# One layer of a hybrid RWKV-7 and S5 network: GELUs ordered behind placed copies, and four smaller reorderings

## The chip, the core and the metric

The kernel runs on one core of a Trainium2 chip. The core has five engines, each with its own queue of instructions that it works off in order: TensorE (PE; its weight loads, PEld, overlap its matmuls), VectorE (DVE), ScalarE (ACT), GpSimd (POOL) and SyncE (SP). Here POOL and SP mostly issue DMAs. The metric is the device time of one execution in microseconds. Lines such as L752 are lines of the kernel before.

## The reference, cut to what matters

One layer for 1024 tokens of width 1024, in float32:

```python
h = rms_norm(x, g_mix_pre)
p = h @ w_in                      # RWKV r, k, v and low ranks | S5 input u | two gates
A = rwkv7_branch(p[rwkv])         # state S per head of 64, one step per token:
#   S = S*w + (S a) b^T + v k^T ;  y = S r ;  then head norm, the bonus (r.k.r_k) v, gate
B = s5_branch(p[u])               # 32 groups of 16 channels, 64 complex states, scan over time
#   y = gelu(Re(C s) + D u) ;  y * sigmoid(y @ w_glu + b_glu)
m = sigmoid(gA) * (A @ w_br0) + sigmoid(gB) * (B @ w_br1)
x = x + rms_norm(m @ w_out, g_mix_post)
z = rms_norm(x, g_ffn_pre) @ w_up           # then a causal convolution of width 3
out = x + rms_norm((gelu(gate) * val) @ w_down, g_ffn_post)
```

## The kernel before

All matrices are multiplied in three matmuls per product: the float32 operands are split into a high part (a cast to fp32r, on ACT) and the rest (a subtraction, on DVE), and PE adds high x high, low x high and high x low (L180 to L182). One such group of three, of 128x128 weights on 512 columns, is called a step here. Weights come by DMA into `wf`, and `wh` (L160, ACT) and `wl` (L161, DVE) are their two parts; activations are split in the same way into `hh` and `hl` (L245, L246).

The stages follow one another: the opening (two halves of 512 tokens are loaded, normalised and multiplied for the S5 input, to about 60 us), the S5 scans in four batches beside the rest of the input projection (to 270), the RWKV recurrence in four groups beside gates, the merge and the GLU (to 740), the rest of the mixing and its norms (to 900), the up-projection (to 1290) and the down-projection.

The order on PE is written out. `drive()` runs several generators ("lanes") against a clock of stated times, `self.now`: each `yield` states what the piece just emitted costs and after how long its next piece is ready. When no lane is ready, the next step of the background work (`fill`: gate tiles, merge, GLU, output projection) is emitted. A stated time that is larger puts more fill ahead of the next piece; it does not itself make the chip wait. On the other engines a scheduler decides by priorities, and `add_manual_dep(..., ORDER)` forces one instruction to stand behind another on the same engine.

The places that the change touches:

- The S5 batch (`s5_batch`, L643 to L655): DVE scans the states, which it holds as `z` and `rot`, and PE then sums three matmuls for each of eight groups (L651 the inputs, L652 and L653 the states). The stated time ahead of them is 17.0 for the first batch and 13.0 for the others (L648).
- The Gram products of a group (`rwkv_front`, L745 to L755; two lanes, u = 0 and 1): 32 small matmuls each into two PSUM banks (L752), masked by DVE into `gr` (L754). `self.masked` is a stated time that keeps the lanes from emitting them too close together. At the end of a front one matmul sums for the bonus (L763), DVE multiplies it (L764), and it uses the same rotating banks.
- The inverse of the chunks' triangular matrices (`rwkv_inv`, L810 to L822): DVE eliminates row by row, the result goes to DRAM (`xd`, L815) and back into `gr` (L822) by DMAs that POOL issues.
- The level (`rwkv_level`, L824 to L851), which puts together blocks of 32 into blocks of 64: DVE transposes `gr` (L835), PE multiplies for u = 0 and 1 (L838), ACT copies the results (L839), PE multiplies again (L840), and ACT copies into `gr` (L841). The chain over the tokens' chunks (L870 to L913) begins behind it.
- The merge's GELUs (`s5_y`, L1250 to L1257): POOL issues the load of an S5 result (L1253), ACT applies GELU (L1254) and casts the high part (L1261), DVE subtracts (L1262). They are forced to stand behind `self.squared`, which is the last square that a front emitted (L700). A load of ACT's function table stands ahead of the first of them.
- The opening (`start`): ACT and DVE split the eight tiles of half 0 as they are normalised (L1046, L245, L246), PE multiplies them (L1158), and the weights of the next S5 columns are split meanwhile.
- The end (`down`, L1895 to L1906): of the last eight output tiles, four are summed with the residual on PE: `resid_sum` multiplies the residual by the identity into a bank (L1898), `outputs` adds the scaled tile (L1829, L1831), and ACT copies it out (L1832). The other four are added by DVE (L1729).

Of the kernel before, what the change touches and what calls it, by code (L numbers as in the profile page):

```python
# [73 lines left out]
class Kern:  # L74
# [546 lines left out]
    def s5_batch(self, b, d, ys):  # L621

        nc, V, G, A = self.nc, self.nc.vector, self.nc.gpsimd, self.nc.scalar
        s = self.s5
        mm = nc.tensor.matmul
        ca, cb, cs, sn, toep, wT = (d[n] for n in ("ca", "cb", "cs", "sn", "toep", "wT"))

        u8 = self.u8[b]
        z = self.t4(shape=(128, 8, 128))
        G.memset(z[:, :, 0:1], 0.0)  # L630
        rot = self.t4(shape=(128, 8, 128))
        yield 0, T_US
        p1, p2 = (self.chk().rearrange("p (g n) -> p g n", n=128) for _ in range(2))
        for p, o in ((p1, 0), (p2, 1)):
            for g in range(8):
                mm(p[:, g], wT[:, g, o:o + 2, :], u8[:, g, :], start=g % 4 == 0, stop=True, skip_group_check=True)
        r2 = self.t4(shape=(128, 8, 128))
        V.tensor_tensor(rot, p1, cs, ALU.mult)
        V.tensor_tensor(r2, p2, sn, ALU.mult)
        V.tensor_tensor(rot, rot, r2, ALU.add)  # L640
        for g in range(8):
            gg = b * 8 + g
            V.tensor_tensor_scan(z[:, g, 1:128], s["rho"][:, gg:gg + 1].to_broadcast([128, 127]),  # L643
                                 rot[:, g, 0:127], 0.0, ALU.mult, ALU.add)
        V.tensor_tensor(rot, z, sn, ALU.mult)
        V.tensor_tensor(z, z, cs, ALU.mult)
        y8 = self.t4(shape=(128, 8, 128))
        yield 3.6, T_SCAN if b else T_SCAN0  # L648
        ps = self.chk().rearrange("p (g n) -> p g n", n=128)
        for g in range(8):  # L650
            mm(ps[:, g], toep[:, g], u8[:, g, :], start=g % 4 == 0, stop=False, skip_group_check=True)  # L651
            mm(ps[:, g], ca[:, g, 1:9, :], z[:, g, :], start=False, stop=False, skip_group_check=True)  # L652
            mm(ps[:, g], cb[:, g, 1:9, :], rot[:, g, :], start=False, stop=True, skip_group_check=True)  # L653
        A.copy(y8, ps)
        for th in range(2):  # L655
            A.dma_start(ys[th].rearrange("c g j n -> j c g n"), y8[:, :, th * 64:th * 64 + 64])
        yield 5.4, 0
# [24 lines left out]
    def rwkv_front(self, d, u, i):  # L682
# [81 lines left out]
        V.tensor_tensor(r, pb, v, ALU.mult)  # L764
        nc.gpsimd.dma_start(d["bv"][u], r)
        d["v"][u] = v
        yield 0.55, 1.5

    def rwkv_nat(self, d):
# [54 lines left out]
    def rwkv_level(self, d, spare):  # L824

        A, V = self.nc.scalar, self.nc.vector
        mm = self.nc.tensor.matmul
        gr = d["gr"]
        p0 = self.chk(1).rearrange("p (u c t) -> p u c t", u=2, t=32)
        p0, p1 = [p0[:, u] for u in range(2)], [self.chb().rearrange("p (c t) -> p c t", t=32) for u in range(2)]  # L830
        xz = (self.tg("x", 1, pool=self.rka) if spare else self.tg("ld", NLD)).rearrange("p (u c t) -> p u c t", u=2, t=32)
        top, bot = [[slice(64 * h + o, 64 * h + o + 32) for h in range(2)] for o in (0, 32)]
        t0, t1 = slice(0, 32), slice(32, 64)
        for h, sl in enumerate(top):
            self.levelled = V.transpose(xz[sl].rearrange("p u c t -> p (u c) t"), gr[sl, :, :, h, t0].rearrange("p u c t -> p (u c) t"))  # L835
        yield 0, T_LT
        kw = dict(stop=True, skip_group_check=True)
        steps = ((lambda u, c, h: mm(p1[u][bot[h], c], gr[top[h], u, c, h, t1], xz[top[h], u, c], start=c == 0, **kw),  # L838
                  lambda u, h: A.copy(xz[bot[h], u], p1[u][bot[h], 0:8])),  # L839
                 (lambda u, c, h: mm(p0[u][top[h], c], xz[bot[h], u, c], gr[bot[h], u, c, h, t1], start=c == 0, **kw),  # L840
                  lambda u, h: A.copy(gr[top[h], u, :, h, t1], p0[u][top[h], 0:8])))  # L841
        for step, evict in steps:
            for u in range(2):
                for c in range(8):
                    for h in range(2):
                        step(u, c, h)
                    if c % 4 == 3:
                        yield 0.3, 0.3, 2.0
                for h in range(2):
                    evict(u, h)  # L850
            yield 0, T_LV  # L851

    def rwkv_chain(self, d):
# [319 lines left out]
    def start(self, xp):  # L1173

        tc = self.tc

        def go(gen, n=1):
            for _ in range(n):
                with tc.high_priority(HPN if gen in norms else HPW):
                    next(gen, None)  # L1180
        with tc.high_priority(HPN):
            xs = [self.load_x(0, xp)]
            self.setup()
            norms = [self.norm(0, xs[0], xp)]
            self.idle = self.gmp()
        consts = self.s5_setup()
        with tc.high_priority(HPS):
            next(consts)
        go(norms[0], 5)
        newton = self.newton  # L1190
        self.behind_x = self.last_x

        def first(o, behind=None):
            with tc.high_priority(HPN - HPW):
                r = []
                for b in (2, 3):
                    self.behind_low = behind
                    r.append(self.load_w(self.a["w_in"][14 + b][:, o:o + 512]))
                return r
        p = first(0, (None, newton))  # L1200
        go(norms[0])
        q = first(512, (self.splits[1][0], self.splits[2][1]))
        self.behind_x, self.behind_low = None, (None, None)
        ws = [[(x[0] + y[0], x[1] + y[1]) for x, y in zip(p, q)]]
        with tc.high_priority(HPW):
            xs.append(self.load_x(1, xp))
            norms.append(self.norm(1, xs[1], xp))
        with tc.high_priority(HP):
            self.nc.sync.dma_start(self.csts[:, 128:NCST], self.a["cst"][:, 128:NCST])
            self.s5w = {}  # L1210
            self.s5_load(0)
            self.s5_load(1)
        a = self.s5_in((2, 3), 0, ws[0])
        go(a, 8)
        with tc.high_priority(HPW):
            ws.append(self.s5_ws((0, 1)))
        with tc.high_priority(HPS):
            self.setup_vecs()
            self.newton = newton
            next(consts, None)  # L1220
        go(a)
        b = self.s5_in((0, 1), 0, ws[1])
        go(b)
        for _ in range(4):
            go(norms[1])
            go(b)
        go(norms[1])
        go(b, 1)
        go(norms[1])
        go(b, 3)  # L1230
        c = self.s5_in((0, 1), 1, ws[1])
        go(c, 9)
        for b in range(2):
            self.load_u8(b)
# [446 lines left out]
    def down(self, dq0, dqf, dqt, dqa, dqs, dqb):  # L1681
# [29 lines left out]
        def stage(g):  # L1711
            return wide(dqs, "st", bufs=4)[:, :512 * len(groups[g])]
# [113 lines left out]
        def outputs(th, src, bc, xs, sums={}):  # L1826
            for m in OUTORD[th]:
                y = src[m] if th else stage(0)[:, 0:512]
                V.scalar_tensor_tensor(y, src[m], self.vec("g_ffn_post", m), bc, ALU.mult, ALU.mult)  # L1829
                if m in sums:  # L1830
                    mm(sums[m], self.cst("ident"), y, start=False, stop=True)  # L1831
                    A.copy(y, sums[m])  # L1832
                else:
                    add(y, y, xs[m])
                nc.sync.dma_start(self.out[m * 128:m * 128 + 128, th * 512:th * 512 + 512], y)
        acc = [None, None]
        f = [[None] * NK for _ in range(2)]
        b, x = [bank(m) for m in range(4)], [bank(4 + m) for m in range(4)]
# [57 lines left out]
        def resid_sum(m, b):  # L1896
            sums[m] = bank(b)
            mm(sums[m], self.cst("ident"), d["xs1"][m], start=True, stop=False)  # L1898
        resid_sum(4, 0)
        resid_sum(5, 1)  # L1900
        self.sumsq(ss, last[0], True)
        self.sumsq(ss, acc[1], False)
        for m, b in ((6, 4), (7, 5)):
            resid_sum(m, b)
        y = self.rstd(ss, 1e-6, 1.0 / D)
        bc = bank(3)  # L1906
        self.spread(bc, y)
        outputs(1, f[1], bc, d["xs1"], sums)

    def build(self):  # L1910
# [183 lines left out]
                yield from self.urgent(out)  # L2094


T_SCAN0 = 17.0
T_US, T_TAB0, T_TAB, T_TRIG, T_SCAN = 5.0, 26.0, 20.0, 12.0, 13.0
T_LD, T_LT = 14.0, 3.0
NEVA = 4  # L2100
T_KN, T_BK, T_GR, T_INV, T_LV, T_CH, T_LN, T_LF = 12.0, 10.0, 2.5, 58.0, 1.0, 0.8, 12.0, 12.0
T_X, T_GLU = 3.0, 25.0
T_N0, T_RS, T_N1, T_N2, T_N4, T_N5, T_N3 = 2.5, 4.0, 2.2, 20.0, 1.6, 24.0, 2.0
NET = 5
T_PN = 8.0
# [87 lines left out]
```

## Time and profile before

| what | us |
| --- | --- |
| three runs | 1517.97, 1521.6, 1523.78 |
| median | 1521.6 |
| the profiled execution | 1524.13 |
| its span | 1522.3 |
| PE busy in it | 1469.8 (97%) |
| DVE busy | 1158.5 (76%) |
| ACT busy | 726.6 (48%) |

The span is the time from the first to the last event of the profiled execution; 1.8 us of the device time lie outside it. Times in the views are counted from the span's start. In a row of the timeline stand the start, the duration, the engine, line and operation, the tiles as output<-input, the count of instructions that are joined in the row, and, in brackets, how long the engine was idle before and what released it. A matmul's duration overlaps the next one's.

### The profile page before, as it was taken

Reading aid. Unit: us, or ns where it says so; the run is one execution under the profiler, and the core shown is the slowest. Engines: PE = TensorE matmul, PEld = TensorE weight load, DVE = VectorE, ACT = ScalarE, POOL = GpSimd, SP = SyncE. Lnnn points to the kernel's source line nnn. Section 1 sums busy time; section 2 is a strip of 40 time slices with the busy share of each in tenths; the row PEclk is TensorE's granted clock in tenths of the full one; section 3 lists DMA queues with packets and bytes.
Section 4 is the critical chain, followed back from the end, with each engine's and each line's share of the span. In section 5 each row is a group of like instructions: output and inputs, shape, how many; then the busy total and the mean of one; then the engine's idle time right before and its main releaser. Section 6 shows DMA issues by size and latency. Waiting matters only on the chain.

```text
span 1522.3 us, 23902 instructions
## 1 busy us (share of the span) xinstructions
PE 1469.8 (97%) x8804; PEld 1166.1 (77%) x8804; DVE 1158.5 (76%) x2157; ACT 726.6 (48%) x1209; POOL 180.2 (12%) x340
## 2 busy tenths in 40 slices
PE   7999999999999998999999999999999999999997
PEld 5788787787677675666788778888888887888875
DVE  7989974765655594975767888888888888698767
ACT  5465444331453434556635555555555555444451
POOL 0022111124021232030110010000000000000000
PEclk9999999999999998999999999999999999999999
DMA  6455344444332446452456575233333336944712
GB/s 211 135 154 159 98 139 145 143 135 152 107 124 96 128 120 192 146 167 70 157 189 199 182 242 180 93 108 117 113 110 117 112 109 225 333 154 138 246 59 111
DMA packets 121558, 225.26 MB, mean 148 GB/s; under 512 B 31024, under 2 KB 37168, under 8 KB 121440
## 3 DMA queue, kind: packets, MB, share of 16 engines
q1 hardware_dynamic: 90576, 154.77, 32.5%
q0 software_dynamic: 21024, 64.71, 12.9%
q10 hardware_dynamic: 9840, 4.24, 1.1%
q8 instruction: 69, 1.13, 0.3%
q14 instruction: 49, 0.40, 0.1%
HBM read 164.16 MB, written 57.41 MB: 146 GB/s over the span
## 4 chain that ended last, share of the span: by engine, by line
PE 44%; DVE 4%; DMA 4%; ACT 1%; issue 1%; SPq 0%; DVEq 0%; ACTq 0%
PE d L1779 8%; PE rp L1600 5%; PE rp L1602 5%; PE rp L1601 5%; PE mm L1602 2%; PE mm L1600 2%; PE mm L1601 2%; DMA st<-in_w_down_dram 2%; PE ch L181 1%; PE mm L180 1%; PE ch L182 1%; PE mm L181 1%; PE gm L180 1%; PE ch L180 1%; PE mm L182 1%
## 5 line engine op out<-in xcount | busy, mean ns | idle before, releaser
L180 PE MATMUL gm<-hh,wh 128*128 128x512 f32 x672 | 283.1, 421 | 1.9 <-DVE ev L1057 1.9
L181 PE MATMUL gm<-hl,wh 128*128 128x512 f32 x672 | 264.9, 394 | 0.1
L182 PE MATMUL gm<-hh,wl 128*128 128x512 f32 x672 | 264.7, 394 | 0.0
L160 ACT CAST wh<-wf 128x512 fp32r<-128x512 f32 x181 | 111.9, 619 | 171.5 <-PE gm L181 88.5
L161 DVE TENSOR_TENSOR wl<-wf,wh 128x512 fp32r<-128x512 f32 x181 | 124.3, 690 | 86.5 <-ACT wh L160 84.5
L180 PEld LDWEIGHTS gm<-hh,wh 128*128 128x128 f32 x672 | 127.0, 189 | 34.3 <-issue 4.0
L182 PEld LDWEIGHTS gm<-hh,wl 128*128 128x128 f32 x672 | 127.0, 189 | 28.1
L181 PEld LDWEIGHTS gm<-hl,wh 128*128 128x128 f32 x672 | 127.4, 190 | 22.5 <-DVE hl L246 1.0
L1779 PE MATMUL d<-xh,wl 128*128 128x512 f32 x308 | 113.5, 392 | 2.1 <-DVE wl L246 2.1
L1779 PE MATMUL d<-xh,wh 128*128 128x512 f32 x308 | 113.9, 393 | 1.1 <-DVE zg L1630 1.1
L1779 PE MATMUL d<-xl,wh 128*128 128x512 f32 x308 | 113.4, 392 | 0.6 <-DVE xl L246 0.6
L1600 PE MATMUL rp<-t,h 128*128 128x512 f32 x252 | 98.3, 390 | 1.4 <-ACT p L1614 1.4
L1602 PE MATMUL rp<-t,l 128*128 128x512 f32 x252 | 98.0, 389 | 0.0
L1601 PE MATMUL rp<-t,h 128*128 128x512 f32 x252 | 98.0, 389 | 0.0
L1779 PEld LDWEIGHTS d<-xh,wl 128*128 128x128 f32 x308 | 58.1, 189 | 15.1 <-DVE wl L246 2.9
L1779 PEld LDWEIGHTS d<-xh,wh 128*128 128x128 f32 x308 | 57.8, 189 | 14.2 <-DVE zg L1630 1.5
L246 DVE TENSOR_TENSOR l<-r,h 128x1024 fp32r<-128x1024 f32 (+1 forms) x40 | 38.9, 971 | 38.9 <-ACT h L245 38.9
L1779 PEld LDWEIGHTS d<-xl,wh 128*128 128x128 f32 x308 | 58.2, 189 | 13.2 <-DVE xl L246 0.9
L245 ACT CAST h<-r 128x1024 fp32r<-128x1024 f32 (+1 forms) x40 | 33.9, 849 | 69.5 <-PE rp L1601 67.2
L1621 DVE SCALAR_TENSOR_TENSOR y<-zv,vecs,y 128x1023 f32<-128x1023 f32 (+1 forms) x42 | 53.7, 1280 | 10.2 <-ACT y L1619 10.2
L1600 PEld LDWEIGHTS rp<-t,h 128*128 128x128 f32 x252 | 47.3, 188 | 11.9 <-ACT p L1614 2.2
L1601 PEld LDWEIGHTS rp<-t,h 128*128 128x128 f32 x252 | 47.3, 188 | 9.8
(476 smaller groups left out, 3338.1 us busy)
## 6 DMA issues: line engine op xcount, KB each, us to landing
r<-in_w_up_dram SPq DMA_DIRECT2D x42, 512.0 KB, 3.5
wf<-in_w_in_dram SPq DMA_DIRECT2D x72, 256.0 KB, 3.1
st<-in_w_down_dram SPq DMA_DIRECT2D x55, 256.0 KB, 4.3
st<-ACT SPq DMA_DIRECT2D x44, 256.0 KB, 4.2
ACT<-y POOLq DMA_DIRECT2D x21, 512.0 KB, 2.9
GT<-ev POOLq DMA_DIRECT2D x32, 256.0 KB, 3.5
wf<-in_w_br_dram SPq DMA_DIRECT2D x32, 256.0 KB, 3.4
wf<-in_w_out_dram SPq DMA_DIRECT2D x32, 256.0 KB, 2.8
```

The lines of the kernel that those rows point to most:

```text
L160: self.last_wh = nc.scalar.copy(h[:, :n], f[:, :n])
L161: low = nc.vector.tensor_tensor(l[:, :n], f[:, :n], h[:, :n].bitcast(F32), ALU.subtract)
L180: mm(ps, a, xh[k], start=a0, stop=False)
L181: mm(ps, a, xl[k], start=False, stop=False)
L182: mm(ps, b, xh[k], start=False, stop=z0)
L245: a = self.nc.scalar.copy(hi, x)
L246: self.split_ops = a, (eng or self.nc.vector).tensor_tensor(lo, x, hi.bitcast(F32), ALU.subtract)
L1600: mm(ps, wh[:, c], xh, start=first and k == 0, stop=False, skip_group_check=True)
L1601: mm(ps, wh[:, c], xl, start=False, stop=False, skip_group_check=True)
L1602: mm(ps, wl[:, c], xh, start=False, stop=k == 3, skip_group_check=True)
L1621: V.scalar_tensor_tensor(y[:, lag:], z[:, 0:1024 - lag], self.vec(nme, i), y[:, lag:], ALU.mult, ALU.add)
L1779: mm(ps, w[:, c], y[:, x], start=start and k == 0, stop=stop and k == 2, skip_group_check=True)
```

## The change

It has five parts.

1. The second S5 batch's stated scan time is 15.3 instead of 13.0.
2. After the bonus product, `self.masked` is set to at least 2.2 later than the stated now, so the other lane's Gram products are emitted later.
3. The level's copies become `self.squared`, so the GELUs that are emitted from then on stand behind the last of them on ACT.
4. In the opening, the casts and subtractions of the weights for the S5 columns of groups 0 and 1 stand behind the split of half 0's last tile.
5. At the end, the residual of output 5 is multiplied after the sum of squares, and outputs 0 and 1 go the way of outputs 4 to 7, so that DVE adds only outputs 2 and 3.

```diff
@@ s5_batch
-        yield 3.6, T_SCAN if b else T_SCAN0
+        yield 3.6, T_SCANS[b]
@@ rwkv_front
         d["v"][u] = v
+        self.masked = max(self.masked, self.now + T_PB)
         yield 0.55, 1.5
@@ rwkv_level
                 for h in range(2):
-                    evict(u, h)
+                    self.squared = evict(u, h)
@@ start
         with tc.high_priority(HPW):
+            self.behind_low = self.splits[7]
             ws.append(self.s5_ws((0, 1)))
+            self.behind_low = (None, None)
@@ down
         resid_sum(4, 0)
-        resid_sum(5, 1)
         self.sumsq(ss, last[0], True)
         self.sumsq(ss, acc[1], False)
-        for m, b in ((6, 4), (7, 5)):
+        for m, b in ((5, 1), (6, 4), (7, 5)):
             resid_sum(m, b)
         y = self.rstd(ss, 1e-6, 1.0 / D)
         bc = bank(3)
         self.spread(bc, y)
+        for m, b in ((0, 6), (1, 7)):
+            resid_sum(m, b)
         outputs(1, f[1], bc, d["xs1"], sums)
@@ constants
-T_SCAN0 = 17.0
+T_SCANS = (17.0, 15.3, 13.0, 13.0)
-T_X, T_GLU = 3.0, 25.0
+T_X, T_GLU, T_PB = 3.0, 25.0, 2.2
```

What this does to the order of instructions is larger than the diff. In the changed kernel line numbers are higher by 1 to 4.

On PE, at the first group's second Gram, the bonus matmul (`rp` from `ld` and a constant) and what follows it, before:

```order
1081 L763 MATMUL rp_3038<-ld_2628,csts 128x512
1082 L752 MATMUL rp_3042<-ar_2745,bk_2746 64x128
1083 L752 MATMUL rp_3043<-ar_2745,bk_2746 64x128
1084 L752 MATMUL rp_3042<-ar_2745,bk_2746 64x128
1085 L752 MATMUL rp_3043<-ar_2745,bk_2746 64x128
```

and after (`gm` is a gate tile of the fill):

```order
1081 L763 MATMUL rp_3038<-ld_2628,csts 128x512
1082 L180 MATMUL gm_3021<-hh_858,wh_2859 128x512
1083 L181 MATMUL gm_3021<-hl_859,wh_2859 128x512
1084 L182 MATMUL gm_3021<-hh_858,wl_2860 128x512
1085 L180 MATMUL gm_3021<-hh_863,wh_2859 128x512
1086 L181 MATMUL gm_3021<-hl_864,wh_2859 128x512
1087 L182 MATMUL gm_3021<-hh_863,wl_2860 128x512
1088 L180 MATMUL gm_3021<-hh_868,wh_2859 128x512
1089 L181 MATMUL gm_3021<-hl_869,wh_2859 128x512
1090 L182 MATMUL gm_3021<-hh_868,wl_2860 128x512
1091 L752 MATMUL rp_3064<-ar_2745,bk_2746 64x128
```

Three steps moved in between. The second group has three at the same place; in the third and fourth the Gram products and the pieces of the chain and level are interleaved anew.

On ACT, at the third group's level, before (`ev` are the S5 results under GELU, `x` from `chb` the copies of the level's first half):

```order
423 L1254 ACT_TABLE_LOAD
424 L1254 ACTIVATE ev_6274<-ev_6274 128x512
425 L1254 ACTIVATE ev_6281<-ev_6281 128x512
426 L1261 CAST hh_6277<-ev_6274 128x512
427 L160 CAST wh_6566<-wf_6568 128x512
428 L1261 CAST hh_6284<-ev_6281 128x512
429 L1254 ACTIVATE ev_6336<-ev_6336 128x512
430 L839 COPY x_6155<-chb_6154 32x256
431 L1261 CAST hh_6339<-ev_6336 128x512
432 L839 COPY x_6155<-chb_6153 32x256
433 L839 COPY x_6155<-chb_6154 32x256
434 L839 COPY x_6155<-chb_6153 32x256
```

and after, where two pairs of copies, now L840, stand apart:

```order
426 L160 CAST wh_6556<-wf_6558 128x512
427 L840 COPY x_6164<-chb_6162 32x256 x2
428 L1257 ACT_TABLE_LOAD
429 L1257 ACTIVATE ev_6208<-ev_6208 128x512
430 L1257 ACTIVATE ev_6215<-ev_6215 128x512
431 L1264 CAST hh_6211<-ev_6208 128x512
432 L1264 CAST hh_6218<-ev_6215 128x512
433 L840 COPY x_6164<-chb_6163 32x256 x2
434 L160 CAST wh_6605<-wf_6607 128x512
435 L1257 ACTIVATE ev_6312<-ev_6312 128x512
436 L1264 CAST hh_6315<-ev_6312 128x512
437 L1257 ACTIVATE ev_6319<-ev_6319 128x512
```

The first pair moved ahead of the table load, the second stands behind two GELUs and two casts. The four copies of the level's second half follow behind two more GELUs and casts.

On DVE, at the same level's transposes (`x` from `gr`), before:

```order
990 L754 TENSOR_TENSOR gr_5718<-rp_6100,csts 128x4x128
991 L754 TENSOR_TENSOR gr_5718<-rp_6101,csts 128x4x128
992 L161 TENSOR_TENSOR wl_6352<-wf_6353,wh_6351 128x512
993 L835 STREAM_TRANSPOSE x_6155<-gr_4616 32x512
994 L754 TENSOR_TENSOR gr_5718<-rp_6132,csts 128x4x128
995 L835 STREAM_TRANSPOSE x_6155<-gr_4616 32x512
996 L754 TENSOR_TENSOR gr_5718<-rp_6133,csts 128x4x128
997 L161 TENSOR_TENSOR wl_6507<-wf_6508,wh_6506 128x512
998 L764 TENSOR_TENSOR ld_5728<-rp_6186,ld_6017 128x512
```

and after:

```order
991 L754 TENSOR_TENSOR gr_5724<-rp_6138,csts 128x4x128
992 L754 TENSOR_TENSOR gr_5724<-rp_6139,csts 128x4x128
993 L161 TENSOR_TENSOR wl_6392<-wf_6393,wh_6391 128x512
994 L764 TENSOR_TENSOR ld_5734<-rp_6192,ld_6023 128x512
995 L1287 SCALAR_TENSOR_TENSOR hl_6170<-hl_6170,gm_6178 128x512
996 L161 TENSOR_TENSOR wl_6557<-wf_6558,wh_6556 128x512
997 L836 STREAM_TRANSPOSE x_6164<-gr_4629 32x512 x2
998 L754 TENSOR_TENSOR gr_5724<-rp_6242,csts 128x4x128
```

The transposes moved behind the bonus product, a product of the merge (L1287, L1284 before) and one more `wl`. Further up, eleven DVE instructions of the fourth group's fronts and of weights moved ahead of the inverse's last steps.

## The prediction

> **What bounds the kernel now.** I read the page first, then the list of what TensorE (PE) waits for, then its idle places one after another, and the granted clock in short stretches.
>
> ```profile
> PE 1469.8 (97%) x8804; PEld 1166.1 (77%) x8804; DVE 1158.5 (76%) x2157; ACT 726.6 (48%) x1209; POOL 180.2 (12%) x340
> ```
>
> PE works 1469.8 of the span's 1522.3 us. The change removes no matmul and adds four at the end, so it can win only in the other 52.5 us, or in time that PE is busy but slow. The list of waits says what the first of these is made of (columns: engine and tile waiting, what it waits for; us in total, times, longest).
>
> ```profile
> PE chk L652 <- DVE t L646: 3.9, 2, 2.1
> PE chk L840 <- ACT x L839: 3.8, 2, 3.4
> ...
> PE gm L1158 <- ACT hh L245: 2.7, 3, 1.8
> PE chk L888 <- ACT p L874: 2.4, 4, 0.9
> PE rp L752 <- DVE ld L764: 2.3, 3, 1.3
> ...
> PE chk L901 <- ACT p L874: 1.5, 1, 1.5
> ```
>
> Each row has an edit facing it. L652 is an S5 batch (edit 1), L840 the level's second half, behind the merge's GELUs (edit 3), L1158 the opening (edit 4), L752 the Gram products (edit 2). Together these four rows hold 12.7 us, 0.8% of the time. A result within 0.5% of 1521.6, that is 7.6 us, is about what a measurement of this kernel cannot tell from no change, so the question is how much of them really goes.
>
> The slow work is seen in the granted clock (columns: stretch, its length, busy time of PE, PEld, DVE, ACT, POOL, PEclk, DMA).
>
> ```profile
> 160.00:170.00 10.00, 7.42 (x45) 6.20 (x44) 9.82 (x18) 3.53 (x5) 0.62 (x1) 0.83 0.20 44
> ...
> 590.00:600.00 10.00, 10.00 (x76) 6.24 (x77) 3.45 (x6) 4.37 (x9) 4.97 (x9) 0.50 0.71 178
> ```
>
> After the S5 wait the mean clock is 0.83, so 10 x 0.17 = 1.7 us are lost; after the level's wait it is 0.50 for ten microseconds, so 10 x 0.5 = 5.0 us are lost. Both stand behind an idle place of over 2 us. A wait here costs its own length and then some.
>
> **The change part by part.** The profiled execution took 1524.1 us, its span is 1522.3, and the median of the three runs is 1521.6; I make the sum as a difference and take it from the median.
>
> Edit 4, the opening. All engines, 28 to 32 us:
>
> ```profile
> 28.06 1.28 ACT L160 CAST wh<-wf 128x512 fp32r<-128x512 f32 x2 [1.88 <-DMA wf<-in_w_in_dram]
> ...
> 28.72 1.35 DVE L161 TENSOR_TENSOR wl<-wf,wh 128x512 fp32r<-128x512 f32 x2 [1.39 <-ACT wh L160]
> ...
> 29.99 1.40 DVE L1046 SCALAR_TENSOR_TENSOR x<-x,vecs,chk 128x512 f32<-128x512 f32 x2
> ...
> 30.76 1.28 ACT L245 CAST hh<-x 128x512 fp32r<-128x512 f32 x2 [1.42 <-DVE x L1046]
> ...
> 31.43 0.74 PE L1158 MATMUL gm<-hh,wh 128*128 128x512 f32 x2 [1.78 <-ACT hh L245]
> ```
>
> PE's 1.78 us go back through ACT's hh to DVE's x, which stood behind two wl, which waited 1.39 us for the two wh and, before them, for the weights to arrive. In the changed order x and hh stand ahead of wh and wl: x can start about 2.6 us earlier (1.39 of waiting and the two wl's 1.35, less the overlap), and 1.78 is covered. The price is that the first wh now comes after hh, around 29.5; PE reaches these L1158 at 31.43 - 1.78 = 29.65 and needs the wh only behind six pairs of them, of about half a microsecond each, around 32.5. Norm 1, which shares ACT and DVE there, may give a part back. At least 0.5 should stay, at most 1.8; I take -1.4.
>
> Edit 1, the second S5 batch. PE, 160 to 171 us and, for the length of a step, 298 to 299:
>
> ```profile
> 164.32 0.49 PE L651 MATMUL chk<-u,t 128*128 128x128 f32 x2 [0.52 <-ACT wT L582]
> 166.87 0.77 PE L652 MATMUL chk<-t,ca 128*128 128x128 f32 x2 [2.06 <-DVE t L646]
> ```
>
> ```profile
> 298.22 0.39 PE L180 MATMUL gm<-hh,wh 128*128 128x512 f32 x1
> ...
> 298.90 0.39 PE L180 MATMUL gm<-hh,wh 128*128 128x512 f32 x1
> ```
>
> A step of three matmuls takes 298.90 - 298.22 = 0.68 us. The stated time grows by 2.3, but in PE's written order only one step moves ahead of the batch: 2.06 - 0.68 = 1.38 of the wait stays, and the 0.52 before it is there too or is covered. So -0.7 is sure. Whether the slow stretch behind it (1.7) goes is open. The opening's 1.78 left no slow clock, as the stretch around it shows, while 2.06 with 0.52 ahead of it did:
>
> ```profile
> 20.00:40.00 20.00, 17.81 (x75) 13.31 (x75) 18.56 (x48) 14.18 (x26) 0.00 (x0) 1.00 0.56 179
> ```
>
> The remaining 1.38 is nearer to the first. Ends -0.7 and -2.4; I take -2.0, most of it.
>
> The Trainium skill, page "TensorE: Matmul & The Clock Gate", section "What's actually happening", has the clock halved after an idle window of about 3.4 us, in windows of 3413 ns that run freely. The trace agrees that slow stretches stand behind idle places; that one of 2.06 us is enough says that a window need not be wholly idle, and where an idle place falls in it will matter.
>
> Edit 2, the Gram products. DVE and PE, 298 to 303 us, and PE at 358:
>
> ```profile
> 300.81 0.68 DVE L764 TENSOR_TENSOR ld<-rp,ld 128x512 f32<-128x512 f32 x1
> ```
>
> ```profile
> 301.55 1.10 PE L752 MATMUL rp<-ar,bk 64*64 64x128 f32 x30 [0.58 <-DVE ld L764]
> ```
>
> ```profile
> 357.92 1.10 PE L752 MATMUL rp<-ar,bk 64*64 64x128 f32 x30 [1.32 <-DVE ld L764]
> ```
>
> The Gram's third matmul needs the bank that the bonus product L764 reads. Three steps, 2.04 us, now stand between them in the first two groups, more than 0.58 and 1.32. The fill is work that PE has to do anyway, and some is taken from a later place. The third instance (2.3 - 0.58 - 1.32 = 0.4) is in the re-interleaved third group. Ends -0.6 and -2.3; I take -2.0.
>
> Edit 3, the third group's level. Five engines, in order of time:
>
> ```profile
> 559.21 0.19 DVE L812 TENSOR_TENSOR x<-x,tm 128x16 f32<-128x16 f32 x1
> ```
>
> ```profile
> 565.79 4.64 POOL L822 DMA_DIRECT2D gr<-xd  x8 [1.09 <-DMA xd<-x]
> ```
>
> ```profile
> 571.66 0.69 DVE L835 STREAM_TRANSPOSE x<-gr 32x512 f32<-32x512 f32 x1
> ```
>
> ```profile
> 576.10 0.44 PE L838 MATMUL chb<-x,gr 32*32 32x32 f32 x16
> ...
> 589.28 0.24 PE L840 MATMUL chk<-gr,x 32*32 32x32 f32 x2 [3.42 <-ACT x L839]
> ...
> 600.81 0.45 PE L870 MATMUL chk<-UV,gr 64*64 64x64 f32 x8
> ```
>
> ```profile
> 581.66 1.28 ACT L1254 ACT_TABLE_LOAD   x1 [6.03 <-issue]
> 582.96 1.38 ACT L1254 ACTIVATE ev<-ev 128x512 f32<-128x512 f32 x2
> 584.24 1.09 ACT L1261 CAST hh<-ev 128x512 fp32r<-128x512 f32 x1
> ...
> 588.86 1.02 ACT L839 COPY x<-chb 32x256 f32<-32x256 f32 x3
> ```
>
> From the level's first matmul to the chain's first (L870) pass 24.7 us, of them 3.8 of waits and 5.0 of slow clock: 15.9 of work. ACT idles 6.03 before the GELUs' table, starts them when their load has come, and the level's copies, ready long before, stand behind them. That is the wait that the edit is aimed at.
>
> The order after the change removes it only in part. First, the two copies of the level's first half now stand ahead of the table, but the other two stand behind the table, two GELUs and two casts: 1.28 + 1.38 + 2 x 1.09 = 4.8 us from about 581.7, so to 586.5. Then wh, two more GELUs and two casts (some 4.2) stand ahead of the first copy of the second half, the one that PE's third group of L840 needs: it ends around 591. Second, the level's transposes come later. On DVE eleven instructions of the fourth group's fronts, 0.6 to 0.7 us each, some 7.5 in all, now stand ahead of the inverse's last step; the stores and loads of the inverse follow it on POOL, and the transposes, 571.66 before, can come at about 579. They stand behind a product of the merge (L1284) and a wl, too. PE comes to the level two steps later than before, at about 577.5, and waits until both transposes are done, about 580.6: 3.1 us. The second place, PE reaching the third L840 group around 589 against 591, costs some 2. So 15.9 + 3.1 + 2 = 21.0, and half of one or two slow stretches of 3.4 us on top (1.7 to 3.4; the 5.0 above are three of them): 22.7 to 24.4 against 24.7. I take -1.0. The best end is that all 3.8 and 5.0 go, -8.8; the worst that the transposes cost 5, the second copies 4 and the clock 5 again, +5.2.
>
> The Trainium skill, page "ScalarE: Activation LUTs", section "What ACT_TABLE_LOAD costs", puts a drain beside the table's own time and comes to about 2.7 us for both; here the table took 1.28 and the GELU began 0.02 later, but with 6 us of idle ahead. Now that copies stand right ahead of it, that would be 1.4 us more for the level's other two copies, by an estimate from that page.
>
> The fourth group's level (L888 and L901 in the list above: 0.9 and 1.5 at 685 and 690) has the same edit from the other side: GELUs and casts move between the level's copies and out of the chain's way. What the chain wins, the level's second copies can lose: between -2.4 and +3, I take -0.3.
>
> Edit 5, the end. PE, ACT and DVE after the last products:
>
> ```profile
> 1507.06 1.96 PE L1898 MATMUL d<-A,csts 128*128 128x512 f32 x4
> ...
> 1509.62 1.16 PE L290 MATMUL d<-csts,rsy 128*128 128x128 f32 x8 [0.60 <-DVE rsy L143]
> 1511.62 3.70 PE L1831 MATMUL d<-r,csts 128*128 128x512 f32 x8 [0.84 <-DVE r L1829]
> ```
>
> ```profile
> 1515.36 0.58 ACT L1832 COPY r<-d 128x512 f32<-128x512 f32 x1 [0.27 <-PE d L1831]
> ```
>
> ```profile
> 1517.30 1.29 DVE L1729 TENSOR_TENSOR q<-q,A 128x512 f32<-128x512 f32 x2
> ```
>
> DVE ends at 1518.6 now. Two adds (1.29) leave it: 1517.3. But PE gets longer: one residual (1.96 / 2 = 0.98) moves behind the squares and fills the 0.60, pushing L290 by 0.4; two residuals then stand ahead of L1831, which ends its wait of 0.84 and starts about 1.3 later, at 1512.9; six outputs at 3.70 / 4 = 0.93 end at 1518.5, and the last copy at 1519.1. That is 0.5 later than 1518.6. Ends: -1.3 (DVE decides) and +1.2; I take +0.5.
>
> Sum: -1.4 - 2.0 - 2.0 - 1.0 - 0.3 + 0.5 = -6.2, so 1521.6 - 6.2 = 1515.4 us, or 1517.9 for an execution like the profiled one.
>
> **The rivals.** *Full relief at the level* (0.26). If DVE has enough slack that the transposes come in time, the level loses both its wait and its slow clock, -8.8 in place of -1.0: -14.0, 1507.6. For it speaks that DVE is busy for only 3.45 of the 10 us from 590 on, so it can catch up; against it the queue order on DVE, POOL and ACT.
>
> *Waits shift and little stays* (0.17). The S5 wait keeps its slow stretch (-0.7), the opening's gain is eaten by the first S5 batch, which waits 1.8 for DVE already (-0.4), the fill that covers the Gram is missed later (-0.9), and the level is even: -2.0, 1519.6. DVE's 9.82 of 10 us at 160 speaks for it. A change that moves fill without removing a wait would look like this too. [...]
>
> *Slower: the level becomes the new wait* (0.07). If the transposes and the second copies come as late as their queues allow, the third group costs +5.2 and the fourth +3; a slow stretch in the fourth adds 1.7, the end 1.2, and the small gains of the last case, 2.0, stand against 11.1: +9.1, 1530.7. It decides from the point at which the losses at the two levels pass the 5 or 6 us won elsewhere.
>
> **How the numbers follow.** My forecast, 1515.4, has 0.50, with a range of its own of 1511 to 1520. A quarter of it lies below 1521.6 - 7.6 = 1514.0: 0.12, with full relief's 0.26 gives faster 0.38. Same is the other 0.38, the 0.17 and 0.01 of the slower case: 0.56. Slower has 0.06. The range runs from 1506.5, just below full relief, to 1524, leaving out the slower case and tails.
>
> **What would show it.** Right: no wait of L1158 near 30; L652's second wait near 1.4 and a clock of 1.0 behind it; no wait of L752 for L764; at the level, PE waiting for the DVE transposes and then for the second copies, with some clock of 0.5 behind. Wrong: no wait at all between level and chain at 577 to 601 (then full relief), the wait for the transposes over 5 us (then slower), or DVE still last at the end.

## The result and the profile after

| | median us | runs | ratio to before (95% interval) |
| --- | --- | --- | --- |
| before | 1522.07 | 10 | 1 |
| changed | 1533.87 | 10 | 1.0075 (1.0054 to 1.0096) |

The change makes the kernel slower, by 0.75% or 11.4 us; the prediction said 6.2 us faster, with a range that ended at 1524. Here and below a difference in measured time is worked out from the ratios. The profiled execution of the changed kernel took 1533.07 us, its span is 1531.3. The page, engine by engine:

```profile
PE 1474.5 (96%) x8812; PEld 1171.8 (77%) x8812; DVE 1158.3 (76%) x2155; ACT 727.3 (47%) x1211; POOL 180.5 (12%) x340
```

The span grew by 9.0 us: PE is busy for 4.7 us more and idle for 4.3 more (56.8 against 52.5). But the page has eight matmuls more (the four that edit 5 adds stand there as two each), and these take 3.7 of the 4.7: the residual sums 5.7 us instead of 3.8, the scaled tiles 5.5 instead of 3.7. The loss is seen better up to the first matmul of the up-projection, because ahead of it both kernels have the same 6288. Before, then after (columns as in the prediction):

```profile
0.00:935.06 935.06, 896.09 (x6288) 696.64 (x6289) 684.06 (x1603) 443.72 (x855) 158.09 (x299) 0.99 0.49 150
```

```profile
0.00:945.46 945.46, 899.77 (x6288) 701.78 (x6289) 685.25 (x1603) 443.32 (x855) 158.35 (x299) 0.98 0.48 149
```

The up-projection starts 10.4 us later. PE is idle for 6.7 us more by then (45.7 against 39.0) and takes 3.7 us more for the same matmuls, at a lower mean clock. So about two thirds of the loss are waits. What PE waits for, by total:

```profile
PE chk L889 <- DVE S L914: 5.4, 2, 5.0
PE chb L839 <- DVE x L836: 4.9, 2, 4.1
PE chk L652 <- DVE t L646: 3.9, 2, 2.1
...
PE chb L900 <- DVE p L892: 2.8, 3, 2.3
...
PE rp L969 <- DVE yn L961: 2.3, 1, 2.3
```

Of the four rows that faced the edits, two are gone from the top (the hh of the opening and the Gram's `ld`), one is untouched (L652), and the level's has changed its name: PE now waits for the level's transposes on DVE instead of for the copies on ACT. Three rows are new, all of DVE, with their long waits between 516 and 675 us: the chain's state S, the chain's p, and the output's yn. PE at the three places (start, duration, and in brackets the idle time and its releaser):

```profile
521.20 0.69 PE L889 MATMUL chk<-S,ar 64*64 64x64 f32 x8 [5.01 <-DVE S L914]
```

```profile
584.44 0.31 PE L839 MATMUL chb<-x,gr 32*32 32x32 f32 x2 [4.08 <-DVE x L836]
585.53 0.63 PE L839 MATMUL chb<-x,gr 32*32 32x32 f32 x14 [0.78 <-DVE x L836]
...
605.19 0.45 PE L871 MATMUL chk<-UV,gr 64*64 64x64 f32 x8
```

The chain starts at 605.19, against 600.81 before. The clock in stretches around them (columns as in the prediction):

```profile
124.00:134.00 10.00, 8.16 (x53) 7.76 (x52) 9.83 (x15) 0.69 (x1) 0.54 (x1) 0.83 0.45 96
```

```profile
515.00:530.00 15.00, 9.99 (x76) 6.99 (x74) 4.31 (x11) 4.35 (x12) 0.71 (x3) 0.89 0.29 87
...
660.00:690.00 30.00, 27.75 (x230) 21.05 (x228) 23.83 (x49) 16.34 (x36) 7.88 (x15) 0.94 0.53 172
```

```profile
576.00:606.00 30.00, 24.78 (x252) 16.75 (x251) 15.22 (x21) 14.52 (x24) 15.64 (x28) 0.77 0.49 150
```

At the level the mean clock is 0.77 over 30 us, so 6.9 us are lost there, more than the 5.0 of before. New slow places are behind the first S5 batch (1.7 us), behind the chain's wait (1.7), after 670 (1.8) and near 862 (1.7); one near 1453 (1.7) is gone.

Why the chain waited at 516 is seen on DVE:

```profile
512.41 0.28 DVE L903 COPY UV<-chb 64x128 f32<-64x128 f32 x1 [0.86 <-PE chb L900]
519.65 1.22 DVE L718 TENSOR_TENSOR_SCAN ld<-csts,ld 128x512 f32<-128x512 f32 x1 [6.96 <-DMA ld<-TZ]
520.80 0.45 DVE L914 SCALAR_TENSOR_TENSOR S<-chb,pt,spt 128x64 f32<-128x64 f32 x2
```

The scan of the fourth group's decays waits 6.96 us for its load, and the chain's state update stands behind it. The same two in the kernel before:

```profile
518.31 1.23 DVE L718 TENSOR_TENSOR_SCAN ld<-csts,ld 128x512 f32<-128x512 f32 x1 [3.11 <-DMA ld<-TZ]
519.46 0.45 DVE L913 SCALAR_TENSOR_TENSOR S<-chb,pt,spt 128x64 f32<-128x64 f32 x2
```

The order is the same. Before, DVE came to the scan 2.5 us later (515.2 against 512.7) and the load landed 1.3 us earlier, so PE lost only 0.6. PE has the same six steps between the chain's product ahead of this and L889 in both kernels. And why the transposes were late, on DVE and POOL:

```profile
569.77 0.18 DVE L813 TENSOR_TENSOR x<-x,tm 128x16 f32<-128x16 f32 x1
...
583.68 0.70 DVE L836 STREAM_TRANSPOSE x<-gr 32x512 f32<-32x512 f32 x1 [2.00 <-DMA gr<-xd]
```

```profile
572.46 1.92 POOL L816 DMA_DIRECT2D xd<-x  x3 [1.58 <-issue]
576.91 0.59 POOL L760 DMA_DIRECT2D md<-gr  x1 [2.53 <-DVE gr L754]
578.90 4.61 POOL L823 DMA_DIRECT2D gr<-xd  x8 [1.40 <-DMA xd<-x]
```

The inverse's last step came at 569.77 instead of 559.21, 10.6 us later: its first came 4.3 us later (531.9 against 527.6), and from first to last it took 37.9 us instead of 31.6. Its loads went out at 578.90 instead of 565.79, and the transposes waited for them.

### The profile page after: what moved, and what is told of

It is laid out like the page before. It is cut to its first block, busy times and chain, and to the rows that moved or that the text cites. A ratio compares the mean times of both kernels' runs of the same rounds, so it can differ in the third digit from the quotient of the medians.

```text
span 1531.3 us, 23909 instructions
## 1 busy us (share of the span) xinstructions
PE 1474.5 (96%) x8812; PEld 1171.8 (77%) x8812; DVE 1158.3 (76%) x2155; ACT 727.3 (47%) x1211; POOL 180.5 (12%) x340
## 4 chain that ended last, share of the span: by engine, by line
PE 72%; DVE 11%; DMA 6%; issue 6%; ACT 3%; POOL 1%; SPq 0%; ACTq 0%; DVEq 0%; POOLq 0%
PE d L1782 10%; PE gm L180 9%; PE gm L181 7%; PE gm L182 7%; PE rp L1603 5%; PE rp L1604 5%; PE rp L1605 5%; PE mm L1604 2%; PE mm L1603 2%; PE mm L1605 2%; DVE wl L161 1%; DMA st<-in_w_down_dram 1%; PE ch L181 1%; PE ch L182 1%; PE ch L180 1%
```

## The experiments

The questions were which of the five edits costs the time, and by what. Two theories stood against each other: A, that it is edit 2 (the Gram products' stated wait), through the new order of the third and fourth groups; B, that it is edit 3 (GELUs behind the level's copies). Times are medians, the ratio is to the kernel before, measured beside it.

**Edit 2 left out.**

```diff
-        self.masked = max(self.masked, self.now + T_PB)
```

> The changed kernel without the Gram products' stated wait (edit 2); the other four edits stay. Theory A (the loss is made by edit 2: it re-interleaves the third and fourth groups, so that the chain waits 5.0 us for DVE near 516, the level's transposes come late near 580, and slow clock follows): about 1514 us, 18 to 20 faster than the changed kernel and faster than before, and neither the wait of 5.0 nor that of 4.1 is there. Theory B (the loss is made by edit 3: GELUs between the level's copies): about 1531, still slower than before.

Measured: 1526.36 us, 1.0024 (1.0005 to 1.0043). Against the changed kernel's 1.0075 that is 7.8 us less, but still slower than before. The waits near 516 and for the transposes are gone, as A said; the time of about 1514 was not reached. Both theories have a part.

**Edit 2 alone.**

```diff
+        self.masked = max(self.masked, self.now + T_PB)
```

> The kernel before with edit 2 alone. Theory A: slower than before by 8 to 12 us, near 1532, with the wait for the chain's state near 516 and the late transposes near 580, as in the changed kernel. Theory B: about 1519.5, faster by the 2.1 us of the Gram waits.

Measured: 1533.14 us, 1.0055 (1.0034 to 1.0075), 8.4 us slower. PE's waits from 500 to 605 us:

```profile
PE chb L839 <- DVE x L836: 5.7, 2, 5.2
PE chk L889 <- DVE S L914: 4.5, 1, 4.5
```

One stated number, without any of the other edits, makes both waits. A holds here.

**Edit 3 alone.**

```diff
-                    evict(u, h)
+                    self.squared = evict(u, h)
```

> The kernel before with edit 3 alone; PE's order is that of before. Theory A: faster than before by 4 to 9 us (the level's 3.8 us of waits and the 5.0 of slow clock at 586 to 600 go, some of it returns as later GELUs), so 1513 to 1518. Theory B: slower, 1528 to 1532, with waits for the level's second copies.

Measured: 1527.36 us, 1.0030 (1.0010 to 1.0050), 4.6 us slower. Neither expectation met it: A said faster, and B's range began at 1528. PE's waits from 574 to 605, then from 605 to 645, then from 645 to 700:

```profile
PE chk L840 <- ACT gr L841: 3.0, 1, 3.0
PE rp L763 <- DVE gr L754: 0.9, 1, 0.9
```

```profile
PE chb L899 <- DVE p L891: 2.2, 1, 2.2
```

```profile
PE rp L968 <- DVE yn L960: 3.9, 2, 3.1
...
PE chk L888 <- ACT p L874: 1.6, 1, 1.6
PE chk L840 <- ACT gr L841: 1.1, 1, 1.1
```

PE's order is that of before. The wait of 3.42 for the level's first copies became one of 3.0 for its second copies (into `gr`): the GELUs still stand on ACT ahead of a copy. The two waits behind it, for p and yn, are new. In both, DVE does the merge's work ahead of what PE waits for. Near 622, with edit 3 alone and then before:

```profile
620.66 1.10 DVE L1274 SCALAR_TENSOR_TENSOR ev<-ev,ev 128x512 f32<-128x512 f32 x1
...
621.85 0.68 DVE L1284 SCALAR_TENSOR_TENSOR hl<-hl,gm 128x512 f32<-128x512 f32 x1
622.45 0.68 DVE L161 TENSOR_TENSOR wl<-wf,wh 128x512 fp32r<-128x512 f32 x1
...
623.26 0.68 DVE L251 SCALAR_TENSOR_TENSOR hl<-ev,hh 128x512 fp32r<-128x512 f32 x1
...
624.08 0.28 DVE L891 TENSOR_TENSOR p<-p,chk 128x128 f32<-128x128 f32 x1
```

```profile
620.87 0.28 DVE L891 TENSOR_TENSOR p<-p,chk 128x128 f32<-128x128 f32 x1
...
621.24 1.09 DVE L1274 SCALAR_TENSOR_TENSOR ev<-ev,ev 128x512 f32<-128x512 f32 x1
```

The chain's p (L891) now stands behind a GLU product, a gate product, a `wl` and a split.

**Edit 2 in the first two groups only**, the other edits as in the change.

```diff
+        if i < 2:
+            self.masked = max(self.masked, self.now + T_PB)
```

> The changed kernel with edit 2 in the first two groups alone. Theory A in its narrow form (what is harmful is the wait in the third group, not what follows from the first two): about 1512, with the 2 us of the first two groups won as well. Theory A in its wide form (three steps taken from the fill early shift everything that follows): 1525 to 1533. Theory B: about 1531.

Measured: 1532.29 us, 1.0060 (1.0038 to 1.0081). The narrow form of A falls: the wait stated in the third group isn't needed. Three steps of fill taken early in the first two groups shift the order from the third group on enough, and PE waits 3.8 us for the chain and 3.5 for the transposes there.

**The inverse ahead of the fronts.** In the changed kernel, the fourth group's normalised keys are ordered behind the third group's inverse on DVE.

```diff
+            self.natted = V.tensor_tensor(x[:, :, 0:ns, q + 1:32], x[:, :, 0:ns, q + 1:32], tv, ALU.add)
...
+        if i == 3:
+            self.tc.add_manual_dep(normed.ins, self.natted.ins.name, ORDER)
```

> The changed kernel, with the fourth group's normalised keys forced behind the third group's inverse on DVE, so that the inverse ends as early in DVE's order as before. Theory of the late inverse (the wait of 4.1 us for the level's transposes near 580 comes from fronts standing ahead of the inverse on DVE): that wait falls below 1.5, the slow clock of 13.7 us behind it shortens, 4 to 9 us faster than the changed kernel, 1525 to 1530. Rival (the queue of POOL's DMAs or the bonus and merge products ahead of the transposes set it): the wait stays near 4 and the time near 1534.

Measured: 1528.96 us, 1.0041 (1.0023 to 1.0060), 5.2 us less than the changed kernel; the two intervals only just overlap. PE's waits from 500 to 605:

```profile
PE chk L891 <- DVE S L916: 4.6, 1, 4.6
PE rp L754 <- DVE bk L743: 3.5, 2, 2.0
```

The wait for the transposes is gone, but PE doesn't come to the level's first matmul any earlier (584.5 us, against 584.4): a part is paid ahead of it. The fourth group's Gram products now wait 3.5 us, against 1.1 in the changed kernel, for the operands that were moved behind, and the clock is 0.83 on average from 560 to 580. What is won lies between the level and the chain, which starts at 601.0 instead of 605.2, at a clock of 1.00 from 580 on. So DVE's order costs time; how much of it by the wait and how much by the clock behind the wait, the run doesn't say.

**The scan behind the chain's state.** In the changed kernel one DVE instruction moves by one place.

```diff
+        if u and i == 3:
+            self.tc.add_manual_dep(scan.ins, self.states[-3].ins.name, ORDER)
```

> The changed kernel, with one instruction moved by one place on DVE: the scan of the fourth group's decays (u = 1), which waits for a load, goes behind the chain's state update instead of ahead of it. Theory of the blocked queue (the 5.0 us near 516 are a chain update standing behind a scan that waits for its load): the wait falls below 1, the slow clock at 521 goes, 4 to 6.5 us faster than the changed kernel, 1527 to 1530. Rival (the fronts of the fourth group are what counts, and they come later now): what is won near 516 is lost before 605, the time stays within 1.5 of 1534.

Measured: 1532.28 us, 1.0064 (1.0039 to 1.0088). The 1.7 us to the changed kernel lie inside both intervals. DVE there:

```profile
516.45 0.48 DVE L916 SCALAR_TENSOR_TENSOR S<-chb,pt,spt 128x64 f32<-128x64 f32 x2 [2.03 <-PE chb L914]
520.89 1.22 DVE L718 TENSOR_TENSOR_SCAN ld<-csts,ld 128x512 f32<-128x512 f32 x1 [3.96 <-DMA ld<-TZ]
522.03 0.26 DVE L894 TENSOR_TENSOR p<-p,chk 128x128 f32<-128x128 f32 x1
```

The state update is free, the wait for it is gone, and the chain's next step, p, is caught behind the same scan: PE waits 2.5 us for it instead of 5.0 for S. The blocked queue is shown; that removing it wins time is not. PE makes the chain's product 3.4 us earlier (517.8 against 521.2) and yet comes to the level's first matmul at the same time (584.6 against 584.4), as the rival said: the level has to wait for the inverse.

**Both of these.**

> The changed kernel with both of these. If the two theories hold and the places are independent: 8 to 15 us faster than the changed kernel, 1519 to 1526, and what is left over the kernel before is the cost of edit 3 further on. If one feeds the other, no better than the better of the two alone.

Measured: 1528.85 us, 1.0042 (1.0024 to 1.0059), no better than the first alone. In its profile PE waits 1.8 us for the transposes again, 2.4 for p and 2.5 for the Gram's operands.

**Edits 1, 4 and 5 only.**

> The kernel before with edits 1, 4 and 5 only. By adding up the runs so far (without edit 2: 1.0024; edit 3 alone: 1.0030) they are worth about -1 us: 1519 to 1522. If the gains of the opening (1.9) and of the S5 batch (0.5) stayed whole, 1519; if the slow clock behind the first S5 batch takes the opening's gain, 1521.5.

Measured: 1523.93 us, 0.9997 (0.9979 to 1.0015): no difference. The parts add up: edit 2 +0.55%, edit 3 +0.30%, the other three -0.03% make 0.82% against the 0.75% (0.54 to 0.96) measured for all.

**Edit 3 in the third level only.**

```diff
+                    last = evict(u, h)
+                    if spare:
+                        self.squared = last
```

> The kernel before with edit 3 in the third group's level only; the fourth group's level leaves its GELUs where they were. If edit 3's loss (1.0030 alone) is made by the third group (the wait passed on to the level's second copies, and DVE's order behind it: 2.2 us near 622, 3.1 near 668): still 3 to 5 us slower than before, 1525 to 1527. If it is made by the fourth group's level (1.1 at 687, 1.6 at 693): no slower than before, 1521 to 1523.

Measured: 1527.72 us, 1.0043 (1.0028 to 1.0058), no less than edit 3 in both levels. The loss is made by the third group's level and what follows it, and not by the fourth's.

**GELUs behind all copies.** Edits 1, 4 and 5, edit 3 in the third level, and the merge's first GELUs written two gate tiles later, so that all of them come behind the level's last copy.

```diff
-MGAP = 3
-XS0 = {1: (0, 1), 2: (2, 3)}
+MGAP = 5
+XS0 = {3: (0, 1), 4: (2, 3)}
```

> Edits 1, 4 and 5, edit 3 in the third level only, and the merge's first GELUs written two gate tiles later, so that they stand behind all of the level's copies on ACT, and not between them. If the wait at the level comes from GELUs standing ahead of any of its copies: the waits of 3.4 or 3.0 us near 586 to 593 fall below 0.5 and the slow clock behind them goes, 4 to 9 us faster than before unless the GELUs now hold up the chain or the merge: 1514 to 1520. If the GELUs' place only chooses who waits: the wait appears at the chain's first copies or at the merge, 1521 to 1526.

Measured: 1529.35 us, 1.0053 (1.0034 to 1.0072). PE's waits from 574 to 605 us, and from 605 on:

```profile
PE chk L890 <- ACT p L876: 4.6, 1, 4.6
```

```profile
PE gm L180 <- ACT hh L250: 5.3, 1, 5.3
```

No wait is left at the level. The chain's first copy waits instead, behind the table, GELUs and casts, and 5.3 us more are waited for a GLU tile's split that comes later now.

**The same, four gate tiles later.**

> As the run before, with the merge's first GELUs four gate tiles later instead of two. The level's copies stand alike; what differs is how the GLU tiles fall into the chain. Same expectation for the level; 1514 to 1520 if the level decides, 1521 to 1528 if the later GLU tiles meet the end of the fourth group's chain.

Measured: 1534.14 us, 1.0084 (1.0068 to 1.0101). The 4.6 at the chain is the same. What is lost over the run before lies between the third group's output and the fourth group's chain, which are 27.2 us apart instead of 18.2; PE waits 3.8 us there for yn.

**The loads on another queue.** The kernel before, with the merge's first four S5 loads on SP.

```diff
-                y = self.s5_y(self.ev(s8), b, 0)
+                y = self.s5_y(self.ev(s8), b, 0, self.nc.sync)
```

> The kernel before, without any of the five edits, with one change: the merge's first four S5 loads are issued by SP, whose queue is free from about 574 on, instead of POOL, where they stand behind the Gram products' stores. The orders on PE, ACT and DVE stay as they were but for a few neighbours. If the level's wait is made by ACT idling for those loads (6.0 us ahead of the table) with the copies queued behind: the loads land 2 to 4 us earlier, the wait of 3.4 us falls by as much, and with it part of the slow clock: 3 to 8 us faster than before, 1514 to 1519. If ACT's work itself (some 8 us of GELUs and casts), not the load, is what holds the copies: the wait stays at 3 or more and the time at 1522.

Measured: 1523.12 us, 1.0004 (0.9984 to 1.0024). ACT at the level:

```profile
583.06 1.28 ACT L1254 ACT_TABLE_LOAD   x1 [7.59 <-DMA ev<-YU]
```

The loads did not come earlier but 1.4 us later, 583.06 against 581.66. PE's waits at the level grew about as much, from 3.8 to 5.3 us in all. So ACT is held by that load, which the row names, and a later load makes a longer wait; whether an earlier one would shorten it, no run shows.

## Why the prediction was wrong, point by point

**The step that failed is the cost of edit 2's fill.** The prediction said that the three steps in front of the Gram products are "work that PE has to do anyway" and put the term at -2.0, with no price for what follows. At the place itself that was right: no wait for the bonus product is left in the first two groups, and PE comes to a product of the second group's chain at 503.6 us instead of 506.1, with two steps more done. But the stated clock that places every later piece has moved, and the orders of the third and fourth groups with it. From that product to the first matmul of the third level, before and then after:

```profile
506.10:576.10 70.00, 67.95 (x489) 52.64 (x488) 52.50 (x164) 30.06 (x64) 20.37 (x40) 1.00 0.50 144
```

```profile
503.60:584.40 80.80, 69.75 (x491) 53.86 (x490) 54.54 (x167) 30.27 (x65) 20.85 (x40) 0.97 0.46 143
```

PE is idle there for about 11 us instead of 2, with next to the same matmuls. Above all these are the 5.0 for the state update and the 4.1 for the transposes. PE did not run out of fill at the state update: six steps stand ahead of it in both kernels, but DVE came earlier to a scan whose load landed later. And the inverse began later and had more of the fourth group's fronts among its last steps, so that the level began later. Edit 2 alone measures +8.4 us. In the changed kernel, ordering the inverse first gave back 5.2; freeing the state update gave back nothing that can be measured. The prediction had seen the new interleaving and priced it at nothing. How the rest of the 8.4 comes about stays open.

**The third level.** The mechanism was right: copies between GELUs, and transposes behind the inverse. Counted as the prediction counts it, from PE's coming there (580.36) to the chain (605.19), the level took 24.8 us, where 22.7 to 24.4 were put and 24.7 was the time before. So this term was +0.1 for -1.0; the chain's later start, 4.4 us, is what PE lost on its way to the level. Inside the term the first wait was mis-sized, 4.9 us for 3.1. The delay of the inverse was counted in DVE instructions that moved ahead of its end (7.5 us) and came to 10.6, because the inverse also began 4.3 us later. Its own stores then held up its loads: from the end of their last issue to the loads went 4.5 us, against 2.2 before, and POOL idled 1.40 for them. The slow clock was the larger error, 6.9 us where 1.7 to 3.4 were put. The second wait, for the second copies, didn't appear in the changed kernel, where PE came late; with edit 3 alone it did, as 3.0 us. The fourth level, put at -0.3, took 13.7 us instead of 14.7 from its first matmul to the chain.

**What edit 3 does further on** was left out. Its price of -1.0 was that of the level, and it costs +4.6 alone, none of it in the fourth level. From the third group's chain to the fourth level, before and then with edit 3 alone:

```profile
600.80:669.40 68.60, 66.70 (x617) 48.34 (x616) 57.72 (x169) 38.41 (x96) 13.60 (x24) 1.00 0.51 146
```

```profile
599.80:677.60 77.80, 70.20 (x617) 50.79 (x616) 61.38 (x172) 38.16 (x97) 13.60 (x24) 0.95 0.47 150
```

PE is idle for 1.9 us before and for 7.6 with edit 3. In the eight profiled kernels that have edit 3 with the GELUs in their old place it is 5.1 to 7.7 us, in the four without it 1.7 to 3.8. So the place is shown. That the two waits near 622 and 668 follow from DVE's order, which the scheduler made anew from there on, is read from the trace; no run put that order back, so this part is argued, not shown.

**S5.** The step did not shorten the 2.06. It went into the idle place ahead of the batch, the 0.52, so the batch began no later as seen from DVE, and the wait inside it stayed; PE and DVE both came 0.7 us earlier. So about -0.5 for -2.0. Without edit 2 (the first experiment) the batch happened to begin 0.3 us later as seen from DVE, and the wait was 1.75: fill shortens it only once the idle place is full. The slow clock stayed in this profile. Of the nine profiled kernels with edit 1 two have it there, of the five without it four; no run has edit 1 alone.

**The opening** was right in size: no wait near 30 is left, and PE reaches the first S5 batch at 125.3 us instead of 127.2. In the profiled execution it was lost again right there; a rival had the wait for DVE eat it, but the wait stayed at 1.84 us and it was the clock that fell behind it.

**The end** was right: from the last product to the end of the span 19.1 us against 18.5, 0.6 later where 0.5 was put. In six of the nine profiled kernels that have edit 5 a slow stretch begins between the last product and PE's last matmul, and in none of the five without it.

**The rival on the other side** named the third level as the new wait and got 0.07. Its 1530.7 lies near the measured time, but partly by luck: it puts the loss at the two levels, and counted as above these took 24.8 us for 24.7 and 13.7 for 14.7. What it had right is that the transposes come as late as the queues allow.

**The table load** at the level, in the changed kernel, right behind two copies:

```profile
588.36 0.75 ACT L840 COPY x<-chb 32x256 f32<-32x256 f32 x2 [7.58 <-PE chb L839]
589.12 1.28 ACT L1257 ACT_TABLE_LOAD   x1
590.42 1.15 ACT L1257 ACTIVATE ev<-ev 128x512 f32<-128x512 f32 x2
```

It starts 0.01 us after the copies end, and the GELU 0.02 after it. The drain that the Trainium skill, page "ScalarE: Activation LUTs", section "What ACT_TABLE_LOAD costs", adds to the load is not seen here, and the 1.4 us of the estimate from it aren't there.

## What to carry to other kernels

In an order that is written out by a stated clock, a number that moves fill has its price at the later places whose order it changes, not only where it is put: follow the order on all engines to the point where both kernels agree again. Where an engine has several microseconds of work that must happen around a critical chain, ordering it behind one link moves the wait to the next link: first copies 3.4 us, second copies 3.0, the chain's copies 4.6. And an instruction that waits for a load blocks whatever stands behind it in its queue; moving one instruction past it leaves the next one caught.

## What the runs showed of the hardware

The slow clock after a wait is partly chance. The kernel before and that with edit 3 alone have the same instructions for the first 570 us, and the same wait of 1.84 us ahead of the first S5 batch. The stretch around it, before and then with edit 3 alone:

```profile
124.00:134.00 10.00, 8.16 (x60) 7.28 (x58) 9.90 (x18) 2.33 (x4) 0.75 (x2) 1.00 0.44 120
```

```profile
124.00:134.00 10.00, 8.15 (x46) 7.54 (x45) 9.86 (x17) 2.30 (x4) 0.71 (x2) 0.83 0.44 113
```

One has the full clock, the other 0.83. Five profiled kernels have the same instructions up to there, and three of them show the slow stretch; of all fourteen, ten do. Up to PE's last matmul, slow stretches are 3.4 us long or a multiple of it. In the changed kernel the second and third begin at 166.2 and 459.7 us, which is 11 and 97 times 3.413 us after the first at 128.6: the slow stretches keep to a raster. An idle place like this one costs 1.7 us or nothing, it seems by where it falls in the raster. That agrees with the freely running window of the Trainium skill, page "TensorE: Matmul & The Clock Gate", section "What's actually happening". With five to ten slow stretches in a profiled execution, that may be a good part of the spread of 15 us between executions of one kernel (1516.83 to 1531.61 for the kernel before).
